# One plain feed-forward block less per layer, with its token sums moved to GpSimd

## The chip, the cores and the metric

The kernel runs on one core of one Trainium2 chip. A core has TensorE (PE, the matrix engine; PEld is its weight load), VectorE (DVE), ScalarE (ACT), GpSimd (POOL) and SyncE (SP), which issues most of the transfers. Each engine works through its own list of instructions in order, and waits on semaphores for the others. The metric is the device time of one execution in microseconds (us), the median of several runs.

## What is computed

Two layers of a decoder trunk over 528 tokens (16 learned meta tokens, then 512 real ones) with a model width of 1024. Each layer has a combined projection, forgetting attention and retention heads, an output projection, and then the part that the change touches, a SwiGLU feed-forward network (FFN) of width 2816:

```
hn = rmsnorm(h, ffn_norm_g)
ff = silu(hn @ w_gate) * (hn @ w_up)
h = h + ff @ w_down
```

After the second layer comes a last norm, and the meta tokens are dropped. All data is float32. Layer 0 works on all 528 tokens in its FFN, layer 1 only on the 512 real ones.

## The kernel before

Activations are held transposed, features on partitions: `h[0..7]` are eight tiles of 128 features by 528 tokens. For precision each float32 operand is split into two float32r tiles, a high part (a cast, on ACT) and a low part (the source less the high part, a subtraction, on DVE or POOL). A product then takes three matmuls: high by high, weight high by activation low, weight low by activation high. So weights arrive by DMA in `raw`, ACT casts them to `whi`, and DVE or POOL subtracts to make `wlo` (`convert`, L165 to L195). A job with `pool` set makes its low parts on POOL, in eight instructions of 128x128; without it DVE makes them in two of 128x512. The high cast of a half (four chunks of 128 rows) always precedes the low parts of that half.

The FFN's 22 blocks of 128 gate and up columns go in rounds (`ROUNDS`, L27): a round makes its blocks' activations, and the next round interleaves the down projection of the round before. There are two kinds of block.

A **plain block** (`dense_steps`, L197) multiplies the eight chunks of the normed input, `xh` and `xl` (made by `scale_split`, L311), by the gate weights in eight steps, and by the up weights in eight more. A step is three matmuls over all tokens, each written as two of 264 columns in layer 0 and one of 512 in layer 1. While a job's steps run, `convert(j + 1, ...)` at steps 1 and 4 makes the two halves of the next job's weights ready.

A **Unit** (L887) computes gate and up for both halves of the tokens with seven half-size products in place of eight, from sums and differences of weight blocks (`make2` to `make4`) and of activation blocks. Each product has four chunks of three matmuls over half of the tokens (264 or 256 columns), 84 matmuls in all. A Unit runs in three parts: head (24 matmuls, needs `xh`, `xl` and the first weights), middle (36, needs the sums `th`, `tl`) and tail (24, needs both).

The activation sums are made once per layer by `x_forms(k)`, k from 0 to 3 (L834), in a buffer `S` of which there are two. ACT scales two token halves of `h[k]` into `S` (L841), four DVE instructions form the four sums (L842 to L845: one subtraction within `S`, three that scale a half of `h[4+k]` and subtract), ACT casts all four to `th`, and DVE makes `tl` (both in `split`, L141). `squares`, `rstd` and `g_done(0)` are inserted between steps as well: the norm's sums of squares, the factor `R` that all later results are scaled by (two matmul pairs at L290, then ACT and DVE), and the first block's gate with its silu, before which ACT loads another function table (L407).

TensorE's order is the order of the program (`manual_schedule`, L1329). For the other engines the framework's scheduler sets the order when the program is built, from the program order, priorities and its own idea of how long things take; on the chip each engine keeps that order even where an instruction in front waits. The first blocks of each layer, f below `PLAIN`, are plain and the other Units. With `PLAIN = 3` the first round, blocks 0 to 2, is plain in whole. Steps counted from 0 at the FFN's start, the x_forms stand ahead of steps 12, 20, 28 and 36, `rstd` ahead of step 12, and the first Unit's head follows the 48 plain steps.

Of the kernel before, what the change touches and what calls it, by code (L numbers as in the profile page):

```python
# [10 lines left out]
F32 = mybir.dt.float32  # L11
F32R = mybir.dt.float32r
AF = mybir.ActivationFunctionType
ALU = mybir.AluOpType

D = 1024
NK = D // 128
# [7 lines left out]
DFF = 2816  # L25
NF = DFF // 128
ROUNDS = ((0, 3), (3, 7), (7, 11), (11, 15), (15, 19), (19, 22))  # L27
PLAIN = 3
HB = NK // 2
EPS = 1e-6  # L30
NBLK = SEQ // 128
# [8 lines left out]
def hybrid_kernel(ctx, tc, x_t, w_in, w_fl, w_out, w_gate, w_up, w_down, vecs, b_fg, rope, decay, mask, ident, out_t):  # L40
    nc = tc.nc
# [9 lines left out]
    h = [state.tile([128, T], F32, name=f"h{k}") for k in range(NK)]  # L51
# [145 lines left out]
    def dense_steps(src, parts, pool=False, banks=False, ahead=(1, 4), own=None, wait=None):  # L197

        j = len(jobs)
        jobs.append({"src": src, "pool": pool, "own": own})

        def chunk(k0, k, n, xs, cols, ps, done):
            def go():
                convert(j)
                if k == 0:
                    t = [psum_a() for _ in cols] if banks else psum()
                    ps.append(t)
                    ps.append(t if banks else [t[:, b] for b in range(2)])  # L210
                size = jobs[j]["w"][0][0]
                _, hi, lo = jobs[j]["w"][(k0 + k) // size]
                wk = (k0 + k) % size
                xh, xl = xs(k)
                for i, (w, x) in enumerate(((hi, xh), (hi, xl), (lo, xh))):
                    for b, (c0, c1) in enumerate(cols):
                        nc.tensor.matmul(ps[1][b][:, 0:c1 - c0], w[:, wk, :], x[:, c0:c1],  # L217
                                         start=(k == 0 and i == 0), stop=(k == n - 1 and i == 2))
                if k == n - 1:
                    done(ps[0]) if wait is None else wait.append(lambda: done(ps[0]))  # L220
                for half, at_step in enumerate(ahead):
                    if k0 + k == at_step:
                        convert(j + 1, 4 * half + 4)
            return go

        steps = []
        for k0, xs, n, cols, done in parts:
            ps = []
            steps += [chunk(k0, k, n, xs, cols, ps, done) for k in range(n)]
        return steps  # L230
# [42 lines left out]
    def fft(tag, dt=F32R, shape=(128, T), bufs=None):  # L273
        return phase["ffn"].tile(list(shape), dt, name=tag, tag=tag, bufs=bufs)
# [72 lines left out]
    def rstd(st, cols, rname="R"):  # L347

        st["R"] = col_rstd(st["parts"], D, cols, rname)
# [443 lines left out]
    def ffn(l, st, real, last):  # L793
        QC = REAL if real else FULL
# [7 lines left out]
        def two(t):  # L802
            return t[:, t0:T].rearrange("p (a b) -> p a b", a=2)
# [4 lines left out]
        def g_done(f):  # L808
            def go(ps):
                sg = tt("sg")  # L810
                if isinstance(ps, list):
                    for v, (c0, c1) in zip(ps, QC):
                        nc.vector.scalar_tensor_tensor(sg[:, c0:c1], v[:, 0:c1 - c0], RSC, st["R"][:, c0:c1],
                                                       ALU.mult, ALU.mult)
                else:
                    nc.vector.scalar_tensor_tensor(sv(sg, real), pv(ps, real), RSC, sv(st["R"], real), ALU.mult, ALU.mult)
                silu(sv(sg, real))
                sgs[f] = sg
            return go

        def u_done(f):
            def go(ps):
                u = tt("tq")
                nc.vector.scalar_tensor_tensor(sv(u, real), pv(ps, real), RSC, sv(st["R"], real), ALU.mult, ALU.mult)
                nc.vector.tensor_mul(sv(u, real), sv(u, real), sv(sgs[f], real))
                fh, fl = act_tile(f)
                split(sv(fh, real), sv(fl, real), sv(u, real))
                acts[f] = (fh, fl)
            return go
# [4 lines left out]
        def x_forms(k):  # L834
            def go():
                if k == 0:
                    st["t"] = [[fft(f"t{p}{i}", shape=(128, 2, 4, w)) for p in "hl"] for i in range(2)]
                s = fft("S", F32, (128, 6, w), 2)
                a, b = ((h[k][:, c0:c1], h[HB + k][:, c0:c1]) for c0, c1 in HC)
                g0, g1 = vcol(V_FFN + l * NK + k), vcol(V_FFN + l * NK + HB + k)  # L840
                nc.scalar.activation(s[:, 0:2], two(h[k]), AF.Copy, scale=g0)  # L841
                nc.vector.tensor_sub(s[:, 2], s[:, 1], s[:, 0])  # L842
                for i in range(2):
                    nc.vector.scalar_tensor_tensor(s[:, 3 + i], b[1], g1, s[:, 1 + i], ALU.mult, ALU.subtract)
                nc.vector.scalar_tensor_tensor(s[:, 5], a[1], g1, s[:, 4], ALU.mult, ALU.subtract)  # L845
                th, tl = (t[:, k % 2] for t in st["t"][k // 2])
                split(th, tl, s[:, 2:6])
            return go
# [180 lines left out]
        for r, (f0, f1) in enumerate(ROUNDS):  # L1029
            for f in range(f0, f1):  # L1030
                if f < PLAIN:
                    steps += dense_steps(w_gate[l, f], [(0, xs, NK, QC, g_done(f) if f else held.append)], banks=f == 1)
                    steps += dense_steps(w_up[l, f], [(0, xs, NK, QC, u_done(f))])
                    continue
                u = Unit(f)
                steps += u.head()
                for v in tails:
                    v.last()
                    steps += v.tail()
                tails = []  # L1040
                u.rest()
                steps += u.middle()
                if fills:
                    p, g0, g1 = fills.pop(0)
                    j = down_job(p, g0, g1)
                    steps += down(j, 0, 2 * p, g0, g1, not real)
                    u.last()
                    steps += u.tail()
                    steps += down(j, 1, 2 * p + 1, g0, g1, False)
                else:  # L1050
                    tails = [u]
            for p, g0, g1 in fills:
                j = down_job(p, g0, g1)
                for s in range(2):
                    steps += down(j, s, 2 * p + s, g0, g1, False)
            fills = [(p, f0, f1) for p in range(NK // 2)]
# [6 lines left out]
        else:  # L1063
# [149 lines left out]
            places = [(end, after_a)] + [(end + n * (i + 1), f) for i, f in enumerate(  # L1213
                (after_0, after_1, after_2, after_3, after_4, after_5, after_6, after_7))]
            steps += merge(rnd, places)
        for i in range(HB):
            steps.insert(NK + 4 + 9 * i, x_forms(i))
        steps.insert(NK + 4, lambda: g_done(0)(held[0]))
        steps.insert(NK + 4, lambda: rstd(st, QC))
        steps.insert(4, lambda: squares(st, QC, False, False))  # L1220
        return steps

    gf = const.tile([128, NK], F32, name="gf")
    nc.vector.tensor_scalar_mul(gf, vec[:, V_FIN:V_FIN + NK], RSC)
# [180 lines left out]
```

## Time and profile before

| what | value |
|---|---|
| median of 3 runs | 1274.08 us (1273.74 to 1275.27) |
| the profiled execution's own time | 1278.19 us |
| its span, first to last instruction | 1276.3 us |
| granted TensorE clock | 0.995 of full speed |
| busy | PE 1258.8, DVE 996.6, ACT 688.2, POOL 265.2 us |
| matmuls | 9271 |

The span is the profiled execution on the chip. A row of a timeline has the start in us from the span's start, the length in us, the engine, the line of the kernel, the operation with what it writes and reads and its size, how many like it follow each other (x), and in brackets how long the engine sat idle before and what ended that. A matmul's row lasts from its start to the end of its pipeline, so neighbours overlap: the pace of TensorE is read from start to start. A row of windows has, for each engine, its busy time in that stretch and in brackets its instructions, then the granted clock. A row of one line's instructions has the shortest, median and longest duration in ns.

### The profile page before, as it was taken

How to read it: one execution, taken by the hardware profiler on the slowest of the kernel's cores; microseconds unless marked ns; L12 is line 12 of the kernel's file. 1: busy time of each engine (PE TensorE's matmuls, PEld its weight loads, DVE VectorE, ACT ScalarE, POOL GpSimd, SP SyncE). 2: the span in 40 equal slices, each digit the busy share in tenths (PEclk: the TensorE clock that was granted, in tenths of full speed). 3: DMA queues.
4: the chain of work that ended last, by engine and by line, in shares of the span. 5: the costliest groups of instructions: out<-in, count | busy, mean ns of one | idle time of the engine just before them, and what ended most of it. 6: DMA issues, size and time to landing. Idle time of an engine off the chain costs nothing.

```text
span 1276.3 us, 23615 instructions
## 1 busy us (share of the span) xinstructions
PE 1258.8 (99%) x9271; PEld 1199.9 (94%) x9271; DVE 996.6 (78%) x1843; ACT 688.2 (54%) x1246; POOL 265.2 (21%) x522
## 2 busy tenths in 40 slices
PE   9999999999999999999999999999999999999997
PEld 8899999999999999999998989999789999999996
DVE  7777856779988887887785777567899888888866
ACT  6666545676444444444464665456764444444444
POOL 3355546420000000000025545554100000000000
PEclk9999999999999999999999999999999999999998
DMA  6322232223333333332323232232224333333321
GB/s 216 93 68 84 79 94 72 74 67 112 108 96 100 100 100 100 100 100 83 102 74 100 76 100 84 75 92 67 99 86 129 100 100 100 100 99 101 106 76 67
DMA packets 45680, 120.57 MB, mean 94 GB/s; under 512 B 5360, under 2 KB 12272, under 8 KB 45568
## 3 DMA queue, kind: packets, MB, share of 16 engines
q1 hardware_dynamic: 45136, 118.77, 29.8%
q8 instruction: 73, 1.20, 0.4%
q14 instruction: 39, 0.32, 0.1%
q10 hardware_dynamic: 432, 0.29, 0.1%
HBM read 116.91 MB, written 2.13 MB: 93 GB/s over the span
## 4 chain that ended last, share of the span: by engine, by line
PE 94%; DVE 2%; ACT 1%; DMA 1%; issue 0%; DVEq 0%; ACTq 0%; SPq 0%
PE psd L217 30%; PE psa L880 18%; PE psd L1015 14%; PE psd L880 13%; PE psa L217 5%; PE psa L1015 4%; PE psa L418 2%; PE psa L572 2%; PE psa L507 2%; PE psa L729 1%; PE psa L699 1%; DMA bc<-cdr 1%; PE psa L379 1%; PE psa L290 0%; DMA cdr<-z 0%
## 5 line engine op out<-in xcount | busy, mean ns | idle before, releaser
L194 POOL TENSOR_TENSOR wlo<-raw,whi 128x128 fp32r<-128x128 f32 x504 | 259.9, 551 | 293.5 <-ACT whi L191 293.5
L217 PE MATMUL psd<-xh,whi 128*128 128x264 f32 (+1 forms) x792 | 197.1, 316 | 0.6 <-ACT whi L191 0.6
L217 PE MATMUL psd<-xh,wlo 128*128 128x264 f32 (+1 forms) x792 | 187.7, 305 | 0.0
L217 PE MATMUL psd<-xl,whi 128*128 128x264 f32 (+1 forms) x792 | 187.3, 304 | 0.4 <-DVE xl L320 0.4
L217 PEld LDWEIGHTS psd<-xh,whi 128*128 128x128 f32 x792 | 129.4, 191 | 5.7 <-ACT whi L191 1.3
L217 PEld LDWEIGHTS psd<-xh,wlo 128*128 128x128 f32 x792 | 128.0, 190 | 6.4 <-DVE wlo L194 0.4
L217 PEld LDWEIGHTS psd<-xl,whi 128*128 128x128 f32 x792 | 128.6, 190 | 4.8 <-DVE xl L320 0.8
L191 ACT CAST whi<-raw 128x512 fp32r<-128x512 f32 (+1 forms) x168 | 98.5, 614 | 51.6 <-PE psd L217 38.2
L868 ACT CAST whi<-raw 128x1024 fp32r<-128x1024 f32 (+2 forms) x62 | 54.9, 886 | 51.0 <-PE psd L880 39.5
L868 ACT CAST fwhi<-raw 128x1024 fp32r<-128x1024 f32 (+2 forms) x62 | 55.7, 898 | 46.6 <-PE psd L880 39.2
L1115 POOL TENSOR_TENSOR th<-th,e 128x544 f32<-128x544 f32 x1 | 1.4, 1370 | 359.1 <-DVE e L1135 359.1
L85 POOL MEMSET kl<- 64x528 f32 x2 | 1.1, 534 | 345.4 <-PE psa L880 345.4
L869 DVE TENSOR_TENSOR wlo<-raw,whi 128x1024 fp32r<-128x1024 f32 (+2 forms) x62 | 62.9, 1015 | 12.1 <-ACT whi L868 12.0
L869 DVE TENSOR_TENSOR fwlo<-raw,fwhi 128x1024 fp32r<-128x1024 f32 (+2 forms) x62 | 64.0, 1032 | 9.6 <-ACT fwhi L868 9.5
L880 PE MATMUL psa<-th,whi 128*128 128x264 f32 (+1 forms) x232 | 65.4, 282 | 0.0
L880 PE MATMUL psa<-th,wlo 128*128 128x264 f32 (+1 forms) x232 | 65.4, 282 | 0.0
L880 PE MATMUL psa<-tl,whi 128*128 128x264 f32 (+1 forms) x232 | 65.3, 282 | 0.0
L880 PE MATMUL psa<-th,fwhi 128*128 128x264 f32 (+1 forms) x224 | 63.4, 283 | 0.0
L880 PE MATMUL psa<-tl,fwhi 128*128 128x264 f32 (+1 forms) x224 | 63.3, 283 | 0.0
L880 PE MATMUL psa<-th,fwlo 128*128 128x264 f32 (+1 forms) x224 | 63.2, 282 | 0.0
L527 ACT ACTIVATE probs<-probs,nmax 128x144 f32<-128x144 f32 (+1 forms) x64 | 36.9, 577 | 47.3 <-DVE nmax L514 34.5
L868 ACT CAST fwhi<-S 128x1024 fp32r<-128x1024 f32 x20 | 21.0, 1050 | 69.1 <-PE psa L880 67.1
(340 smaller groups left out, 4053.7 us busy)
## 6 DMA issues: line engine op xcount, KB each, us to landing
raw<-w_in SPq DMA_DIRECT2D x54, 512.0 KB, 3.5
raw<-w_gate SPq DMA_DIRECT2D x44, 512.0 KB, 3.8
fraw<-w_up SPq DMA_DIRECT2D x38, 512.0 KB, 3.5
raw<-w_down SPq DMA_DIRECT2D x64, 256.0 KB, 2.8
raw<-w_out SPq DMA_DIRECT2D x16, 512.0 KB, 3.4
raw<-w_down SPq DMA_DIRECT2D x32, 192.0 KB, 2.5
bc<-cdr SPq DMA_DIRECT2D x16, 264.0 KB, 3.4
raw<-w_up SPq DMA_DIRECT2D x6, 512.0 KB, 3.6
```

Of the source, the lines that this page charges most:

```text
L191: pin(nc.scalar.copy(hi, job["raw"][:, c0:c1]), pinned)
L194: pin(sub(lo[:, i:i + step], job["raw"][:, c0 + i:c0 + i + step], hi[:, i:i + step].bitcast(F32)), pinned)
L217: nc.tensor.matmul(ps[1][b][:, 0:c1 - c0], w[:, wk, :], x[:, c0:c1], start=(k == 0 and i == 0), stop=(k == n - 1 and i == 2))
L379: nc.tensor.matmul(ps[:, 0:c1 - c0], wf[:, k, :], st["x"][k][part][:, c0:c1], start=(i == 0), stop=(i == 2 * NK - 1))
L418: nc.tensor.transpose(ps[:, 128 * j:128 * j + 128], src[:, o:o + 128], idt)
L507: nc.tensor.matmul(sc[0:nq, 0:c1 - c0], st["q"][s][:, q0:q0 + nq], kk[:, c0:c1], start=(i == 0), stop=(i == 1))
L527: nc.scalar.activation(pr, pr, AF.Exp, bias=nmax[0:nq], scale=-1.0, accum_out=rsum)
L572: nc.tensor.matmul(po[:, c0:SEQ], v[:, j, :], pp[:, j, META + c0:T], start=(j == 0 and i == 0), stop=(j == 4 and i == 1))
L868: nc.scalar.copy(hi, src)
L869: nc.vector.tensor_sub(lo, src, hi.bitcast(F32))
L880: nc.tensor.matmul(bank()[:, 0:b.shape[-1]], a[:, o + k, :], b, start=(fresh and k == 0 and i == 0), stop=(k == n - 1 and i == 2), skip_gr ...
L1015: nc.tensor.matmul(v[:, 0:c1 - c0], a[:, s * n + k, :], b[:, c0:c1], start=(k == 0 and i == 0), stop=(k == n - 1 and i == 2))
```

## The change

`PLAIN` becomes 2: block 2 of each layer is now a Unit too, the first round has two plain blocks and a Unit, and that Unit's head follows 32 plain steps. Of the plain blocks' four weight jobs all but the first get `pool` set, so POOL makes their low parts. In `x_forms` ACT scales both `h[k]` and `h[4+k]` into a larger `S`, and all four sums become POOL subtractions. The x_forms stand ahead of steps 7, 11, 15 and 19, and `rstd` and `g_done(0)` ahead of step 11.

```diff
-PLAIN = 3
+PLAIN = 2
...
-                s = fft("S", F32, (128, 6, w), 2)
-                a, b = ((h[k][:, c0:c1], h[HB + k][:, c0:c1]) for c0, c1 in HC)
+                s = fft("S", F32, (128, 8, w), 2)
                 g0, g1 = vcol(V_FFN + l * NK + k), vcol(V_FFN + l * NK + HB + k)
                 nc.scalar.activation(s[:, 0:2], two(h[k]), AF.Copy, scale=g0)
-                nc.vector.tensor_sub(s[:, 2], s[:, 1], s[:, 0])
+                nc.scalar.activation(s[:, 6:8], two(h[HB + k]), AF.Copy, scale=g1)
+                nc.gpsimd.tensor_sub(s[:, 2], s[:, 1], s[:, 0])
                 for i in range(2):
-                    nc.vector.scalar_tensor_tensor(s[:, 3 + i], b[1], g1, s[:, 1 + i], ALU.mult, ALU.subtract)
-                nc.vector.scalar_tensor_tensor(s[:, 5], a[1], g1, s[:, 4], ALU.mult, ALU.subtract)
+                    nc.gpsimd.tensor_sub(s[:, 3 + i], s[:, 7], s[:, 1 + i])
+                nc.gpsimd.tensor_sub(s[:, 5], s[:, 6], s[:, 4])
...
-                    steps += dense_steps(w_gate[l, f], [(0, xs, NK, QC, g_done(f) if f else held.append)], banks=f == 1)
-                    steps += dense_steps(w_up[l, f], [(0, xs, NK, QC, u_done(f))])
+                    steps += dense_steps(w_gate[l, f], [(0, xs, NK, QC, g_done(f) if f else held.append)], f > 0, f == 1)
+                    steps += dense_steps(w_up[l, f], [(0, xs, NK, QC, u_done(f))], True)
...
-        for i in range(HB):
-            steps.insert(NK + 4 + 9 * i, x_forms(i))
-        steps.insert(NK + 4, lambda: g_done(0)(held[0]))
-        steps.insert(NK + 4, lambda: rstd(st, QC))
-        steps.insert(4, lambda: squares(st, QC, False, False))
-        return steps
+        forms = (7, 11, 15, 19)
+        return merge(steps, [(4, lambda: squares(st, QC, False, False)), (NK + 3, lambda: rstd(st, QC)),
+                             (NK + 3, lambda: g_done(0)(held[0]))], [(p, x_forms(i)) for i, p in enumerate(forms)])
```

The change's lines after `x_forms` are one to three numbers lower than before's; here lines are before's unless a row of the change is shown. Its two ACT scalings are L840 and L841, and its sums L842 to L845 as before.

On GpSimd, at the start of layer 0's FFN, the piece of the difference in which the token sums come in. The `wlo` rows are low parts of weights, eight to a job; the 256 end with those of the first up job, and the later groups of four belong to the second gate job:

```order
-L194 TENSOR_TENSOR wlo<-raw,whi 128x128 x248
-L85 MEMSET kl_8409 64x528
-L85 MEMSET kl_8410 64x528
+L194 TENSOR_TENSOR wlo<-raw,whi 128x128 x256
+L842 TENSOR_TENSOR S<-S 128x264
+L844 TENSOR_TENSOR S<-S 128x264 x2
+L845 TENSOR_TENSOR S<-S 128x264
+L842 TENSOR_TENSOR S<-S 128x264
+L844 TENSOR_TENSOR S<-S 128x264 x2
+L194 TENSOR_TENSOR wlo<-raw,whi 128x128 x4
+L845 TENSOR_TENSOR S<-S 128x264
+L194 TENSOR_TENSOR wlo<-raw,whi 128x128 x4
```

Before, GpSimd had no work there until the next layer's memsets; now it has 24 low parts and 16 sums in the FFN's beginning, mixed in one queue. Behind this piece stand the sums of k = 2, the first sum of k = 3, four low parts of the second up job, two sums, one low part, the last sum, and three low parts.

On ScalarE at the same place, before. `sqh` is the high part of the norm's sum of squares, `R` the norm's factor, `sg` the first gate, and each `x2` of L191 the two halves of one weight job:

```order
L841 ACTIVATE S<-h_74,vec 128x528
L142 CAST sqh<-ss 128x528
L191 CAST whi<-raw 128x512 x2
L295 ACTIVATE R<-psa,epsc 128x264 x2
L142 CAST th_4303<-S 128x1056
L296 ACTIVATE R<-R 128x528
L142 CAST th_4303<-S 128x1056
L191 CAST whi<-raw 128x512 x2
```

On ScalarE now, from the first cast of k = 2's sums to the weights of the first Unit. `ah` is the high part of the first block's product:

```order
L142 CAST th_4256<-S 128x1056
L191 CAST whi<-raw 128x512
L841 ACTIVATE S<-h_80,vec 128x528
L191 CAST whi<-raw 128x512
L142 CAST th_4256<-S 128x1056
L407 ACT_TABLE_LOAD
L407 ACTIVATE sg<-sg 128x528
L868 CAST fwhi<-S 128x1024
L142 CAST ah_4375<-tq 128x528
L868 CAST whi<-raw 128x1024
```

The two L191 rows here are the second up job's high parts. They stand behind the cast of k = 2's sums, and the first Unit's weights (the last row) behind the cast of k = 3's sums, the table load, the first silu, and two more casts.

On VectorE now, from the last low part of the sums to the low parts of the first Unit's weights (the last row):

```order
L143 TENSOR_TENSOR tl_4257<-S,th_4256 128x1056
L915 TENSOR_TENSOR S<-S,raw 128x512
L825 TENSOR_TENSOR tq<-tq,sg 128x528
L921 TENSOR_TENSOR fraw<-raw,fraw 128x512
L813 SCALAR_TENSOR_TENSOR sg<-psa,R 128x264 x2
L143 TENSOR_TENSOR al_4376<-tq,ah_4375 128x528
L869 TENSOR_TENSOR fwlo<-S,fwhi 128x1024
L869 TENSOR_TENSOR wlo<-raw,whi 128x1024
```

Before, only one row stood between the last `tl` and this `wlo`; now six do, the first silu's result among what they wait for. In layer 1 the change puts this `wlo`, and its cast on ScalarE, ahead of the `al` and `fwlo` rows, and keeps the sums of squares' cast behind k = 0's `th`; otherwise the queues are alike.

## The prediction

> **What bounds the kernel now.** I read the page first, then TensorE's timeline at both FFN starts, then windows there, then the other engines' timelines. The page's span, busy time and chain:
>
> ```profile
> span 1276.3 us, 23615 instructions
> PE 1258.8 (99%) x9271; PEld 1199.9 (94%) x9271; DVE 996.6 (78%) x1843; ACT 688.2 (54%) x1246; POOL 265.2 (21%) x522
> PE 94%; DVE 2%; ACT 1%; DMA 1%; issue 0%; DVEq 0%; ACTq 0%; SPq 0%
> ```
>
> TensorE is the bound, so a matmul less is time less, and a wait put into TensorE is time more. Where the change acts, windows of 20 us in the plain blocks of layer 0 and of layer 1 show TensorE without a gap, VectorE full too, GpSimd empty:
>
> ```profile
> 292.00:312.00 20.00, 20.00 (x166) 19.85 (x165) 19.96 (x37) 12.61 (x20) 0.00 (x0) 1.00 0.40 136
> 925.00:945.00 20.00, 20.00 (x87) 16.25 (x88) 19.69 (x36) 12.64 (x19) 0.00 (x0) 1.00 0.32 98
> ```
>
> TensorE's timeline: the first plain step, the Unit's first and twelfth matmul, in each layer.
>
> ```profile
> 290.02 0.41 PE L217 MATMUL psd<-xh,whi 128*128 128x264 f32 x2
> ...
> 325.56 0.28 PE L880 MATMUL psa<-xh,whi 128*128 128x264 f32 x1
> ...
> 326.89 0.28 PE L880 MATMUL psa<-xh,wlo 128*128 128x264 f32 x1
> ...
> 918.08 0.40 PE L217 MATMUL psd<-xh,whi 128*128 128x512 f32 x1
> ...
> 952.61 0.28 PE L880 MATMUL psa<-xh,whi 128*128 128x256 f32 x1
> ...
> 953.92 0.28 PE L880 MATMUL psa<-xh,wlo 128*128 128x256 f32 x1
> ```
>
> **Part one: a plain block becomes a Unit.** In layer 0, 35.54 us hold three blocks of 96 matmuls and the four of L290: 0.1217 each, a block 11.68. Eleven starts of a Unit take 1.33, 0.121 each, so its 84 cost 10.16: 1.52 less. In layer 1 a block is at most a third of 34.53; the window's 87 in 20 us give 0.230 each, and its 48 cost 11.04. A Unit's pace there is 1.31 / 11 = 0.119, and 84 cost 10.0: 1.04 less. Together **-2.6**. Without a wait the first Unit would start one block sooner, at 313.88 and 941.57; its third matmul, which needs the first low part on VectorE, comes two starts later, at 314.12 and 941.81.
>
> **Part two: what GpSimd gets.** Its low parts free and beside VectorE, VectorE's own subtraction with and without GpSimd beside it, GpSimd's one other large subtraction-like instruction, and VectorE beside that; then VectorE's price for a sum:
>
> ```profile
> L194 POOL TENSOR_TENSOR wlo<-raw,whi x504: 447/463/2071, 21.9 to 902.8; 128x128 fp32r<-128x128 f32 x168
> ...
> 21.95 3.39 POOL L194 TENSOR_TENSOR wlo<-raw,whi 128x128 fp32r<-128x128 f32 x8 [20.26 <-ACT whi L191]
> 267.57 2.18 POOL L194 TENSOR_TENSOR wlo<-raw,whi 128x128 fp32r<-128x128 f32 x4 [8.38 <-ACT whi L191]
> 268.07 0.94 DVE L297 TENSOR_TENSOR nwt<-r 128x528 f32<-128x528 f32 x1 [0.37 <-ACT r L296]
> 302.60 0.70 DVE L297 TENSOR_TENSOR nwt<-R 128x528 f32<-128x528 f32 x1
> ...
> 1262.10 0.40 DVE L1111 TENSOR_TENSOR S<-S,sq 128x240 f32<-128x240 f32 x1
> 1262.35 1.37 POOL L1115 TENSOR_TENSOR th<-th,e 128x544 f32<-128x544 f32 x1 [359.05 <-DVE e L1135]
> 1262.73 1.25 DVE L1111 TENSOR_TENSOR S<-S,sq 128x240 f32<-128x240 f32 x1
> ...
> L842 DVE TENSOR_TENSOR S<-S x8: 418/424/429, 297.5 to 938.4; 128x264 f32<-128x264 f32 x4, 128x256 f32<-128x256 f32 x4
> ```
>
> A free low part costs 3.39 / 8 = 0.424. A sum is not in the trace: it lies between 0.424 (as if 264 columns were 128) and 0.463 x 264 / 128 = 0.955 (as if nothing were fixed). On the line through 128 columns (0.463) and 544 (1.37) it is 0.76, and 0.04 less back to back: I take **0.72**, 0.70 for 256 columns. [...]
>
> The two engines also hold each other up. A VectorE instruction with both inputs in SBUF took 0.94 beside GpSimd where it takes 0.70, and one of 0.40 took 1.25, until GpSimd's 1.37 was over; four low parts beside it took 2.18, not 1.70. L299, with an input in PSUM, I count as free of this. So I add the two engines' times where both have such work. [...]
>
> **Part three: the queues at layer 0's start.** The ACT and VectorE rows that I price with:
>
> ```profile
> 289.98 1.15 ACT L191 CAST whi<-raw 128x512 fp32r<-128x512 f32 x2 [0.63 <-PE psd L217]
> 291.03 0.74 ACT L841 ACTIVATE S<-h,vec 128x528 f32<-128x528 f32 x1
> ...
> 300.31 1.07 ACT L142 CAST th<-S 128x1056 fp32r<-128x1056 f32 x1
> ...
> 305.26 1.28 ACT L407 ACT_TABLE_LOAD   x1
> 307.62 0.65 ACT L407 ACTIVATE sg<-sg 128x528 f32<-128x528 f32 x1 [1.08 <-DVE sg L816]
> ...
> 319.78 1.06 ACT L868 CAST whi<-raw 128x1024 fp32r<-128x1024 f32 x1 [1.09 <-issue]
> ```
>
> ```profile
> 291.09 2.12 DVE L320 SCALAR_TENSOR_TENSOR xl<-h,vec,xh 128x528 fp32r<-128x528 f32 x3
> ...
> 301.42 1.26 DVE L143 TENSOR_TENSOR tl<-S,th 128x1056 fp32r<-128x1056 f32 x1
> ...
> 309.61 0.70 DVE L825 TENSOR_TENSOR tq<-tq,sg 128x528 f32<-128x528 f32 x1
> ...
> 310.83 0.43 DVE L813 SCALAR_TENSOR_TENSOR sg<-psa,R 128x264 f32<-128x264 f32 x1
> 311.17 0.70 DVE L143 TENSOR_TENSOR al<-tq,ah 128x528 fp32r<-128x528 f32 x1
> ...
> 319.19 1.25 DVE L143 TENSOR_TENSOR tl<-S,th 128x1056 fp32r<-128x1056 f32 x1
> ...
> 320.98 1.22 DVE L869 TENSOR_TENSOR wlo<-raw,whi 128x1024 fp32r<-128x1024 f32 x1
> 322.11 0.69 DVE L915 TENSOR_TENSOR S<-S,raw 128x512 f32<-128x512 f32 x1
> ```
>
> GpSimd starts when the up job's first half is cast, 290.55. To its last sum stand 21 low parts, 21 x 0.424 = 8.9, and 16 sums, 16 x 0.72 = 11.5: 20.4. On the shared time lie five `xl`, one `ss` and `sql` on VectorE, some 0.66 each (4.6), later a `tl` of 1.2, half of another, two instructions for `R` and one for the Unit's weights (3.7): 8.3. GpSimd also waits for ACT: for k = 1's second scaling, which stands behind k = 0's cast (1.07 + 0.74 less the 0.72 that GpSimd has to do), for k = 2's (0.7), and for the second up job's high part, behind k = 2's cast (1.07 + 0.57 less 0.72): 2.7. The last sum ends at 290.55 + 20.4 + 8.3 + 2.7 = 321.95.
>
> From there, by the queues shown: on ACT cast 1.07, table load 1.28, silu 0.65, 3.0 in all (`tl` and L915 are done by then); on VectorE L825, L921, two L813, `al`, `fwlo`, `wlo`, 0.70 + 0.69 + 0.86 + 0.70 + 1.22 + 1.22 less overlaps, 5.1; ACT's 1.06 for `fwhi`, 0.65 and 1.06 end before. The Unit's third matmul comes at 321.95 + 8.1 = 330.05, against 314.12: **+15.9**. Part of it shows sooner, as waits of the second up job for its high parts, which stand behind k = 2's cast.
>
> Layer 1: GpSimd starts at 918.65 by the like cast; own work 8.9 + 16 x 0.70 = 20.1; shared 6 x 0.66 + 3.0 = 7.0; waits 2.7; the last sum at 948.45. There `wlo` stands ahead of `al` and `fwlo`, so the tail is 3.0 + three instructions of 0.62 + 1.22 = 6.1: 954.55 against 941.81, **+12.7**. L290 waits there too, since the squares' cast stands behind k = 0's, but GpSimd's queue ends later and covers that.
>
> **The clock.** The only longer gap that TensorE has shows what follows one:
>
> ```profile
> 683.42 0.41 PE L418 MATMUL psa<-idt,vt 128*128 128x128 f32 x1 [1.80 <-DVE vv L484]
> 683.48 0.78 PE L217 MATMUL psd<-xh,whi 128*128 128x512 f32 x1
> 684.05 0.63 PE L217 MATMUL psd<-xl,whi 128*128 128x512 f32 x1
> 684.48 0.63 PE L217 MATMUL psd<-xh,wlo 128*128 128x512 f32 x1
> ...
> 686.99 0.40 PE L217 MATMUL psd<-xh,whi 128*128 128x512 f32 x1
> ```
>
> ```profile
> 683.50:686.90 3.40, 3.40 (x11) 2.92 (x12) 2.81 (x10) 0.72 (x2) 0.00 (x0) 0.50 0.43 147
> ```
>
> After 1.80 us of idling the starts lie 0.43 apart, not 0.23, until 686.99, and the granted clock of that window is 0.50. 3.4 us at half pace lose 1.7; once a layer, behind the last wait, that is **+3.4**. Earlier such losses lie inside the waits for GpSimd.
>
> **What is free.** ACT's added scalings, 8 of 0.74, are in the waits above. SP's loads move by a row or two, and TensorE does not wait for one now. VectorE's relief, 16 sums and six half low parts a layer, is worth nothing, since TensorE did not wait for it. The new Unit's product is needed some 6 us behind its tail (36 matmuls of the next Unit and 12 of the down projection, 0.12 each), where block 2's had a head more; I count nothing, and at most 0.4 a layer in the range.
>
> **Sum.** -2.6 + 15.9 + 12.7 + 3.4 = +29.4 on the profiled execution's 1278.2, so 1307.6. Its own time lies 4.1 over the runs' median, 1274.1; I forecast 1303.5. This kernel's measurement can tell 0.2%, 2.5 us, from no change.
>
> **The rivals.**
> - *No sharing.* GpSimd and VectorE do not delay each other here; for it speaks that many low parts keep the median of 463 ns, against it the 1.25 and 2.18. Then 8.3 and 7.0 go: 29.4 - 15.3 = +14, 1288.
> - *Cheap sums.* A sum costs 0.424 and nothing is shared: 16 x 0.30 less again in a layer, +4 to +5, 1279. Against it stands the 1.37.
> - *All hidden, faster.* TensorE's work decides: -2.6, 1271.5. This needs the last sum 8.1 before 314.12, at 306.0: 21 low parts and 16 sums in 15.45, so a sum of at most 0.41 with no wait at all, about VectorE's own 0.424. The other engines' slack speaks for it, every GpSimd row against.
> - *Just covered.* The waits come to 1.3 a layer and eat the gain: 1274.
> - *Sums not sooner.* The places in the program are sooner, but by the queues they end later, 324.3 for the last `tl` (321.95 + 1.07 + 1.26), where before's row above ends at 320.4; this is my forecast itself.
>
> **Chances.** Forecast 0.64 (its own range 1295 to 1313: a sum of 0.955 adds 16 x 0.235 x 2 = 7.5, and the late product 0.8), no sharing 0.19, cheap sums 0.06, all hidden 0.07, just covered 0.04. The range takes the first two: 1286 to 1313, 0.83. Slower 0.88, with most of cheap sums; same 0.05; faster 0.07.
>
> **What would show it.** GpSimd's L842 to L845 at 0.7 or more each, longer where VectorE's `xl` and `tl` run; ACT idle before `th` for GpSimd's S; TensorE idle at the second up job for `whi` and at the first Unit for `wlo`, over 10 us a layer, with a half-clock stretch behind. Sums under 0.5, or TensorE without a gap until the first Unit, would prove me wrong.

## The result and the profile after

The change makes the kernel slower: 1304.07 us median of 4 runs (1302.4 to 1305.29), against 1274.67 (1273.74 to 1276.19) for the kernel before beside it, a ratio of 1.0229 with a 95% interval of 1.0211 to 1.0246. The forecast was 1303.5. The profiled execution's own time is 1304.02, its span 1302.2, its granted clock 0.988.

The page of the change, span, busy times and chain:

```profile
span 1302.2 us, 23752 instructions
PE 1264.3 (97%) x9295; PEld 1202.9 (92%) x9295; DVE 993.5 (76%) x1813; ACT 696.7 (54%) x1260; POOL 321.9 (25%) x602
PE 84%; DVE 6%; POOL 3%; ACT 3%; DMA 2%; issue 1%; ACTq 0%; DVEq 0%; SPq 0%; POOLq 0%
```

TensorE's share of the chain falls from 94% to 84%, and GpSimd, absent before, holds 3%. Where it happens, the windows at the start of layer 0's FFN show (columns as before: length, PE, PEld, DVE, ACT, POOL, granted clock):

```profile
290.00:310.00 20.00, 16.65 (x132) 15.93 (x131) 9.24 (x11) 9.64 (x16) 18.73 (x27) 1.00 0.29 107
310.00:330.00 20.00, 12.60 (x71) 12.21 (x72) 15.10 (x20) 11.04 (x14) 8.14 (x13) 0.74 0.08 23
```

VectorE was full before (19.96 of 20) and now does 9.24: it waits. The full engine is GpSimd, 18.73 of 20. In the second window TensorE has gaps and the granted clock drops to 0.74. TensorE's timeline, with the first plain step of layer 0, its longest wait, the Unit's third matmul, and the same for layer 1, where L290 waits as well (layer 1's attention part starts at 661.15):

```profile
287.86 0.41 PE L217 MATMUL psd<-xh,whi 128*128 128x264 f32 x2
...
315.40 0.78 PE L217 MATMUL psd<-xh,whi 128*128 128x264 f32 x2 [7.35 <-DVE sg L816]
...
325.92 0.39 PE L880 MATMUL psa<-xh,wlo 128*128 128x264 f32 x1 [1.91 <-DVE wlo L869]
...
661.15 0.40 PE L217 MATMUL psd<-xh,whi 128*128 128x512 f32 x1
...
928.96 0.40 PE L217 MATMUL psd<-xh,whi 128*128 128x512 f32 x1
...
940.90 0.71 PE L290 MATMUL psa<-sqh,ones 128*128 128x512 f32 x1 [2.61 <-ACT sqh L142]
...
955.42 0.77 PE L217 MATMUL psd<-xh,whi 128*128 128x512 f32 x1 [2.94 <-DVE sg L816]
...
965.29 0.39 PE L880 MATMUL psa<-xh,wlo 128*128 128x256 f32 x1 [1.07 <-DVE wlo L869]
```

From first plain step to first plain step the span divides into stages. Before, layer 1's attention part starts here:

```profile
647.81 0.40 PE L217 MATMUL psd<-xh,whi 128*128 128x512 f32 x1
```

| stage | before | after | difference |
|---|---|---|---|
| up to layer 0's FFN | 290.02 | 287.86 | -2.2 |
| layer 0's FFN | 357.79 | 373.29 | +15.5 |
| layer 1's attention part | 270.27 | 267.81 | -2.5 |
| layer 1's FFN and the end | 358.22 | 373.24 | +15.0 |

The two FFNs take 30.5 more. The attention parts, which the change does not touch, differ for the most part by TensorE's pace in two short stretches (last section); together they are about the 4.1 by which the profiled execution of before lay over its median.

GpSimd in layer 0, from the first up job's low parts to the last sum and the three low parts behind it, and then the line that ends each form (a form is one `x_forms`), with who waited for it:

```profile
288.57 6.74 POOL L194 TENSOR_TENSOR wlo<-raw,whi 128x128 fp32r<-128x128 f32 x8 [16.49 <-ACT whi L191]
295.27 0.75 POOL L842 TENSOR_TENSOR S<-S 128x264 f32<-128x264 f32 x1
...
300.11 1.90 POOL L844 TENSOR_TENSOR S<-S 128x264 f32<-128x264 f32 x2 [1.11 <-ACT S L841]
301.97 1.70 POOL L194 TENSOR_TENSOR wlo<-raw,whi 128x128 fp32r<-128x128 f32 x4
...
304.34 2.75 POOL L194 TENSOR_TENSOR wlo<-raw,whi 128x128 fp32r<-128x128 f32 x4
...
312.20 3.16 POOL L194 TENSOR_TENSOR wlo<-raw,whi 128x128 fp32r<-128x128 f32 x4 [1.00 <-ACT whi L191]
...
317.14 0.75 POOL L845 TENSOR_TENSOR S<-S 128x264 f32<-128x264 f32 x1
317.85 1.29 POOL L194 TENSOR_TENSOR wlo<-raw,whi 128x128 fp32r<-128x128 f32 x3
```

```profile
L845 POOL TENSOR_TENSOR S<-S x8: 723/735/757, 297.5 to 958.4; 128x264 f32<-128x264 f32 x4, 128x256 f32<-128x256 f32 x4
...
  ACT th L142: 31.4, 8
```

A sum takes 0.75, eight low parts beside VectorE's `xl` 6.74 in place of 3.39, and ScalarE stands idle 31.4 us in front of the eight `th` casts. VectorE's queue inherits this. Its rows up to the `sg` for which TensorE waits 7.35:

```profile
299.43 1.26 DVE L143 TENSOR_TENSOR tl<-S,th 128x1056 fp32r<-128x1056 f32 x1 [4.43 <-ACT th L142]
305.52 1.26 DVE L143 TENSOR_TENSOR tl<-S,th 128x1056 fp32r<-128x1056 f32 x1 [4.83 <-ACT th L142]
307.42 0.96 DVE L297 TENSOR_TENSOR nwt<-R 128x528 f32<-128x528 f32 x1 [0.65 <-ACT R L296]
308.41 0.77 DVE L299 SCALAR_TENSOR_TENSOR nwt<-psa,nwt 128x264 f32<-128x264 f32 x2
311.63 1.26 DVE L143 TENSOR_TENSOR tl<-S,th 128x1056 fp32r<-128x1056 f32 x1 [2.45 <-ACT th L142]
312.81 0.96 DVE L300 SCALAR_TENSOR_TENSOR R<-nwt,R 128x528 f32<-128x528 f32 x1
313.69 0.94 DVE L914 TENSOR_TENSOR S<-fraw 128x512 f32<-128x512 f32 x1
314.56 0.70 DVE L816 SCALAR_TENSOR_TENSOR sg<-psd,R 128x528 f32<-128x528 f32 x1
```

The second up job needs a `psd` buffer, of which there are two; the first gate's product holds one until this `sg` has read it. `sg` needs `R`, and `R`'s last step stands behind k = 2's `tl`, which waits for ScalarE's cast, which waits for GpSimd. The wait bears VectorE's name, its cause is three queues back.

### The profile page after: what moved, and what is told of

The parts are those of the page before. It is cut to its first block, busy times and chain, and to the rows that moved or that the text cites. A ratio compares the mean times of both kernels' runs of the same rounds, so it can differ in the third digit from the quotient of the medians.

```text
span 1302.2 us, 23752 instructions
## 1 busy us (share of the span) xinstructions
PE 1264.3 (97%) x9295; PEld 1202.9 (92%) x9295; DVE 993.5 (76%) x1813; ACT 696.7 (54%) x1260; POOL 321.9 (25%) x602
## 4 chain that ended last, share of the span: by engine, by line
PE 84%; DVE 6%; POOL 3%; ACT 3%; DMA 2%; issue 1%; ACTq 0%; DVEq 0%; SPq 0%; POOLq 0%
PE psd L217 24%; PE psa L880 18%; PE psd L1015 14%; PE psd L880 12%; PE psa L1015 4%; PE psa L217 4%; PE psa L418 2%; POOL wlo L194 2%; PE psa L572 2%; PE psa L507 1%; PE psa L729 1%; PE psa L699 1%; POOL S L844 1%; PE psa L379 1%; DVE fwlo L869 1%
## 5 line engine op out<-in xcount | busy, mean ns | idle before, releaser
L194 POOL TENSOR_TENSOR wlo<-raw,whi 128x128 fp32r<-128x128 f32 x552 | 291.1, 562 | 321.9 <-ACT whi L191 321.8
L217 PE MATMUL psd<-xh,whi 128*128 128x264 f32 (+1 forms) x744 | 185.8, 318 | 10.5 <-DVE sg L816 10.3
L217 PE MATMUL psd<-xl,whi 128*128 128x264 f32 (+1 forms) x744 | 176.2, 305 | 1.6 <-DVE xl L320 1.6
L217 PE MATMUL psd<-xh,wlo 128*128 128x264 f32 (+1 forms) x744 | 175.4, 304 | 0.0
L217 PEld LDWEIGHTS psd<-xh,whi 128*128 128x128 f32 x744 | 122.2, 192 | 15.7 <-issue 7.5
L217 PEld LDWEIGHTS psd<-xl,whi 128*128 128x128 f32 x744 | 121.2, 191 | 7.0 <-DVE xl L320 3.6
L217 PEld LDWEIGHTS psd<-xh,wlo 128*128 128x128 f32 x744 | 120.6, 190 | 5.3
L191 ACT CAST whi<-raw 128x512 fp32r<-128x512 f32 (+1 forms) x160 | 93.8, 612 | 45.5 <-PE psd L217 33.7
L869 DVE TENSOR_TENSOR wlo<-raw,whi 128x1024 fp32r<-128x1024 f32 (+2 forms) x64 | 64.3, 1004 | 13.3 <-ACT whi L868 13.2
L880 PE MATMUL psa<-th,whi 128*128 128x264 f32 (+1 forms) x248 | 69.9, 282 | 1.1 <-ACT e L946 1.1
L946 ACT COPY e<-psa 128x264 f32<-128x264 f32 (+1 forms) x120 | 45.0, 375 | 30.5 <-PE psa L880 26.2
```

Source lines behind the costliest of these rows:

```text
L191: pin(nc.scalar.copy(hi, job["raw"][:, c0:c1]), pinned)
L194: pin(sub(lo[:, i:i + step], job["raw"][:, c0 + i:c0 + i + step], hi[:, i:i + step].bitcast(F32)), pinned)
L869: nc.vector.tensor_sub(lo, src, hi.bitcast(F32))
L880: nc.tensor.matmul(bank()[:, 0:b.shape[-1]], a[:, o + k, :], b, start=(fresh and k == 0 and i == 0), stop=(k == n - 1 and i == 2), skip_gr ...
L946: nc.scalar.copy(self.t["e"][:, i], self.t["x"][:, 0:w])
```

## The experiments

**Theory.** GpSimd's one queue of 24 low parts and 16 sums, lengthened by what GpSimd and VectorE take from each other (eight low parts in 6.74 us, not 3.39), runs late; ScalarE's casts and VectorE's rows behind them inherit that, and TensorE waits in the second plain block and at the first Unit. A "shared port" in the expectations is the author's name for this taking; the runs show what it costs, not where in the hardware it arises. **Rivals:** B, one of the two kinds of work is the whole cost; C, the Unit cannot be fed 11.7 us sooner whoever does the work; F, the PSUM buffer or the order on VectorE is the cost.

First the change with one kind of work, or both, given back to VectorE. **Sums on VectorE:**

```diff
...
-                nc.gpsimd.tensor_sub(s[:, 2], s[:, 1], s[:, 0])
+                nc.vector.tensor_sub(s[:, 2], s[:, 1], s[:, 0])
...
-                    nc.gpsimd.tensor_sub(s[:, 3 + i], s[:, 7], s[:, 1 + i])
+                    nc.vector.scalar_tensor_tensor(s[:, 3 + i], b[1], g1, s[:, 1 + i], ALU.mult, ALU.subtract)
...
```

> The change, but the sixteen token sums of a layer go back to VectorE in the form of the kernel before (0.424 us each there); the low parts stay on GpSimd, the first round stays two plain blocks and a Unit, the places stay sooner. Theory A (GpSimd's mixed queue of 24 low parts and 16 sums sets the first Unit's start): GpSimd has only 8.9 us of low parts up to the last sum, so its part of the wait goes; VectorE takes 16 x 0.424 = 6.8 us a layer back, some 26 us of work ahead of the first Unit against 24 us of TensorE work, so 0 to 6 us of waiting a layer are left: 1272 to 1284 us. Rival B (the low parts of the plain blocks are the cost): little changes, 1297 or more. Rival C (a Unit 11.7 us sooner cannot be fed by ScalarE and VectorE, whoever makes the sums): 1290 or more, with ScalarE never waiting for GpSimd's S.

Measured: 1287.12, ratio to before 1.0089 (1.0077 to 1.0102). More than half of the loss goes, less than A expected.

**Low parts on VectorE:**

```diff
-                    steps += dense_steps(w_gate[l, f], [(0, xs, NK, QC, g_done(f) if f else held.append)], f > 0, f == 1)
-                    steps += dense_steps(w_up[l, f], [(0, xs, NK, QC, u_done(f))], True)
+                    steps += dense_steps(w_gate[l, f], [(0, xs, NK, QC, g_done(f) if f else held.append)], banks=f == 1)
+                    steps += dense_steps(w_up[l, f], [(0, xs, NK, QC, u_done(f))])
```

> The change, but the plain blocks' weight low parts go back to VectorE; the sums stay on GpSimd. Theory A: GpSimd's queue loses 21 x 0.424 = 8.9 us and some of the shared time, VectorE gains six halves of two low parts (7.4 us a layer): of about 15 us of waiting a layer 4 to 8 are left, 1282 to 1292 us. Rival B (the low parts are the cost): no waiting left, 1272 to 1275. Rival C (the Unit cannot be fed sooner, whoever does it): as the change, 1298 or more.

Measured: 1290.77, 1.0116 (1.0102 to 1.013), as A expected. B falls: with either kind alone on GpSimd some 40 to 50% of the 29.4 stays, so neither is the whole cost.

**Both on VectorE:**

> The change with both kinds of work back on VectorE, sums and low parts: two plain blocks and the sooner places alone, GpSimd empty there. Theory A (the first Unit waits for the longest queue): VectorE then has some 33 us ahead of the first Unit against 24 of TensorE, 8 to 10 us of waiting a layer, 1288 to 1292 us; better than the change, worse than with either half on GpSimd. Rival C (the sooner Unit is the cost whoever does the work): 1300 or more. If GpSimd's queue were the only cost: 1272.

Measured: 1290.24, 1.0108 (1.0092 to 1.0123). A's number, though not A's order (the run with the sums on GpSimd is no quicker), and C in part: without GpSimd 14.5 us stay. In this kernel's windows VectorE has hardly a gap, and TensorE has:

```profile
293.00:313.00 20.00, 18.83 (x152) 18.25 (x151) 20.00 (x39) 12.25 (x18) 0.00 (x0) 1.00 0.22 74
313.00:333.00 20.00, 17.93 (x146) 17.50 (x145) 19.94 (x28) 10.89 (x16) 0.00 (x0) 1.00 0.30 93
```

In the plain blocks and Units TensorE waits most for VectorE's `wlo` (3.0 us in all), then for ScalarE's `fwhi` (2.6) and `ah` (2.3). A full VectorE is the likely reason for the 14.5; that it is the only one is not shown.

**The kernel before with the sums alone on GpSimd** (the change's `x_forms`, nothing else):

> The kernel before (three plain blocks, old places, low parts on VectorE) with one edit: the sums go to GpSimd and ScalarE scales both halves, as in the change. Theory A: a GpSimd sum still costs 0.72 or more, but it stands alone in its queue and the first Unit comes 11.7 us later than in the change, so TensorE does not wait: 1272 to 1277 us. Rival D (a sum on GpSimd makes each form's chain too long wherever it stands, its four sums of 0.75 with ScalarE's second scaling in front of every cast): 5 us or more a layer, 1284 or more.

Measured: 1288.46, 1.0094 (1.0078 to 1.0109). The theory's number is wrong and rival D's right: 11.7 us more room does not cover GpSimd's sums. Whether the chain that D names is the cost is open, since what the two engines take from each other can cost as much (13.3 us in the next run). ScalarE waits for the sums there, in us, times and longest:

```profile
ACT th L142 <- POOL S L845: 17.8, 8, 3.1
```

The next run was made to see why. It puts sixteen subtractions a layer on GpSimd for which **nobody waits**, beside VectorE's own sums:

```diff
+                d = fft("D", F32, (128, 4, w), 1)
+                for i in range(4):
+                    c0, c1 = HC[i % 2]
+                    nc.gpsimd.tensor_sub(d[:, i], h[k][:, c0:c1], h[HB + k][:, c0:c1])
```

> The kernel before, and beside it sixteen GpSimd subtractions a layer of the sums' size (h[k] less h[4+k], half of the tokens each), four at each form, into a tile that nothing reads: no engine waits for them, so only what the two engines take from each other costs. Shared-port theory: VectorE is full there (19.69 of 20 us in the kernel before) and loses some 0.3 to 0.6 us to each, 5 to 9 us a layer, of which TensorE's slack of a few us swallows a part: 4 to 16 us in all, 1280 to 1292 us. Without sharing: 1275 to 1278, no wait of TensorE that the kernel before has not.

Measured: 1288.77, 1.0101 (1.0085 to 1.0116), 13.3 us for work that nothing reads. ScalarE's and VectorE's instructions stand in the same order as before at both FFN starts, so no queue was rearranged. TensorE's largest wait, the subtraction's durations (ns), three `xl` of VectorE beside it and a subtraction of VectorE of the same size alone, then windows of layer 0, the second behind the waits:

```profile
PE psd L217 <- DVE xl L320: 7.1, 7, 2.0
...
L849 POOL TENSOR_TENSOR D<-h,h x32: 721/1188/1273, 280.8 to 932.6; 128x264 f32<-128x264 f32 x16, 128x256 f32<-128x256 f32 x16
...
293.81 3.67 DVE L320 SCALAR_TENSOR_TENSOR xl<-h,vec,xh 128x528 fp32r<-128x528 f32 x3
297.41 1.25 DVE L340 TENSOR_TENSOR ss<-ss,sq 128x528 f32<-128x528 f32 x1
...
300.43 0.70 DVE L143 TENSOR_TENSOR sql<-ss,sqh 128x528 fp32r<-128x528 f32 x1
```

```profile
288.00:299.00 11.00, 7.33 (x46) 6.13 (x44) 11.00 (x12) 5.15 (x9) 10.84 (x10) 0.92 0.39 143
...
297.15:303.95 6.80, 6.06 (x26) 5.45 (x26) 6.39 (x10) 1.77 (x3) 2.12 (x2) 0.50 0.11 16
```

Both engines look busy to the brim, but each finishes one instruction in 1.2 us (3.60 / 3 on VectorE, a median of 1.188 on GpSimd) where alone they take 0.70 and 0.72: they nearly take turns. No engine waits for these subtractions, so that is what the two engines take from each other, and it costs as much as GpSimd's real sums did. Only a part of the 13.3 is waiting: TensorE idles 7.1 for `xl`, and the granted clock is 0.50 for 6.8 us in each layer behind that. TensorE works 6.06 of them in layer 0 and 5.26 in layer 1, which at half pace loses, by estimate, another 5.7. These subtractions ran some microseconds sooner than the change's sums, beside `xl`; the size carries over only roughly.

**The places alone**, three plain blocks and all on VectorE:

> The kernel before (three plain blocks, sums and low parts on VectorE) with the sooner places alone. Theory A (the places only reorder ScalarE's and VectorE's queues; the cost of the change without GpSimd is that the first Unit comes 11.7 us sooner): 1274 to 1279 us. Rival C2 (the sooner places hold up R and the second plain block): 1285 or more, as the change without GpSimd's work had 1290.

Measured: 1279.07, 1.0022 (1.0012 to 1.0031). At the upper end of what A expected; the places are a small cost, not a gain.

**The change with three plain blocks:**

```diff
-PLAIN = 2
+PLAIN = 3
...
-                    steps += dense_steps(w_gate[l, f], [(0, xs, NK, QC, g_done(f) if f else held.append)], f > 0, f == 1)
-                    steps += dense_steps(w_up[l, f], [(0, xs, NK, QC, u_done(f))], True)
+                    steps += dense_steps(w_gate[l, f], [(0, xs, NK, QC, g_done(f) if f else held.append)], f == 1, f == 1)
+                    steps += dense_steps(w_up[l, f], [(0, xs, NK, QC, u_done(f))], f < 2)
```

> The change with three plain blocks (block 2 plain as before, its low parts on VectorE): sums and 24 low parts a layer on GpSimd, sooner places. If the first Unit's start alone decides, as my prediction priced it (ready 43.8 us after layer 0's FFN start in the prediction, some 39.6 in the change's trace, against 35.5 of TensorE work), 4 to 6 us of waiting are left over both layers, 1279 to 1283 us. If GpSimd's queue holds up TensorE already before the Unit (the second up job, which stands at the same place here), the waits of the change's second block stay, 8.7 in layer 0 and 6 in layer 1 with some half-clock time behind them: 1290 to 1296 us.

(Its 43.8 and 39.6 are misread: by the rows quoted, the third matmul of the Unit comes 40.0 after the FFN's start in the prediction and 38.1 in the change. The bound that it draws from them changes little.) Measured: 1301.86, 1.0193 (1.0179 to 1.0207), beyond both. Block 2 is plain again, and 25 of the 29 us stay. TensorE's wait is where it was in the change, and as long:

```profile
315.78 0.78 PE L217 MATMUL psd<-xh,whi 128*128 128x264 f32 x2 [7.32 <-DVE sg L816]
```

The first Unit waits for nothing here: its third matmul comes 48.94 and 45.99 after the FFN's start (337.18 - 288.24 and 975.84 - 929.85), 13.2 and 11.2 later than without a wait, all of it lost before the Unit. So the waits in the second plain block are hard costs of their own; here they are not a share, shown early, of a wait that the Unit would have anyway.

**One kind of work with three plain blocks,** first the low parts:

> Three plain blocks, sooner places, the sums on VectorE, only the low parts of blocks 0 and 1 on GpSimd (24 a layer). From the run with two plain blocks, where low parts on GpSimd gained 3 us over all on VectorE, and the run of the sooner places alone (1279): if the low parts relieve VectorE, 1275 to 1278; if the shared port takes back more than the relief where TensorE had no wait, 1280 to 1284.

Measured: 1280.03, 1.0035 (1.0022 to 1.0048), at the lower edge of the second range; over the places alone it is too little to tell. And the sums:

> Three plain blocks, sooner places, only the sums on GpSimd, low parts on VectorE. As with the old places (1288): 1286 to 1291 if the chain of GpSimd's sum, ScalarE's th and VectorE's tl, all in order, is what costs; 1280 or less if the old places were a part of it. The sum of what sums alone and low parts alone cost, against the 1302 of both, says how much comes from the two standing in one queue.

Measured: 1287.54, 1.0094 (1.008 to 1.0107), as with the old places. That fits the chain and the taking of turns alike; the run does not separate them. All eight, in us over the kernel before measured beside each, sooner places throughout, each uncertain by 1 to 2:

| on GpSimd | three plain blocks | two plain blocks |
|---|---|---|
| nothing | +2.5 | +14.5 |
| low parts | +4.5 | +11.3 |
| sums | +12.0 | +15.0 |
| both | +25.3 | +29.4 |

With three plain blocks the sums add 9.5 and the low parts 2.0, both together 22.8: 11.3 come only with the two in one queue (half-clock stretches behind the longer waits included: behind the 7.32 at 315.78 pairs of matmuls start 0.44 apart). With two, where VectorE is full, each alone costs about what VectorE doing it costs (-3.2 and +0.5), and both add 14.9. The missing block costs 12.0 where VectorE does all and 4.1 where GpSimd does both: the waits overlap, and no single part owns the 29.4.

**The PSUM wait.** The second up job's product into the single banks, so that no `sg` must come first:

```diff
...
-                    steps += dense_steps(w_up[l, f], [(0, xs, NK, QC, u_done(f))], True)
+                    steps += dense_steps(w_up[l, f], [(0, xs, NK, QC, u_done(f))], True, f == 1)
```

VectorE then reads that product in two instructions, one for each bank.

> The change, but the second up job writes into the single PSUM banks (psa), so it need not wait until VectorE's first sg has emptied a psd bank; that is the wait of 7.4 us in layer 0 and 2.9 in layer 1. Theory A (the release is late only because all queues run behind GpSimd's sums): the wait moves to the second up job's low parts and to the first Unit's wlo, total within 3 us of the change, 1301 to 1305 us. Rival F (VectorE's order, with sg behind k = 2's tl, is the cost): 8 to 10 us go, 1294 to 1296.

Measured: 1305.66, 1.0225 (1.0211 to 1.0239): nothing gained, F falls. TensorE's waits in layer 0 there:

```profile
315.18 0.81 PE L217 MATMUL psa<-xh,whi 128*128 128x264 f32 x2 [4.11 <-ACT whi L191]
326.54 0.39 PE L885 MATMUL psa<-xh,whi 128*128 128x264 f32 x1 [2.30 <-ACT whi L873]
328.96 0.59 PE L885 MATMUL psa<-xh,wlo 128*128 128x264 f32 x1 [1.91 <-DVE wlo L874]
```

With the buffer free the same job waits 4.11 for its high part, which stands behind k = 2's cast, and the Unit gives back the rest: its third matmul comes 38.11 and 36.37 after the FFN's start (328.96 - 290.85 and 968.32 - 931.95), in the change 38.06 and 36.33. In the change the wait for the buffer is thus a share of the Unit's wait. With three plain blocks the buffer was not freed; how much of the 25.3 it costs there is open.

**A fifth sum:**

```diff
+                nc.gpsimd.tensor_sub(s[:, 1], s[:, 6], s[:, 0])
```

> The change with a fifth GpSimd subtraction of the same size in each of the four forms of a layer, whose result nothing reads; ScalarE's and VectorE's queues keep their order. Theory A (GpSimd's queue sets when the middle of the plain blocks and the first Unit can run): 4 x 0.75 = 3.0 us a layer on GpSimd, up to 4 with what it holds up on VectorE: 6 to 8 us more than the change, 1310 to 1313 us. Rival E (GpSimd has slack and VectorE's or ScalarE's own queue sets it): 0 to 2 us more.

Measured: 1308.11, 1.0244 (1.023 to 1.0257), against the change's 1.0229: 1.9 us more, with intervals that overlap. That number lies in E's range, not in A's. By the traces layer 0's FFN takes 375.46 in place of 373.29, 2.2 more, and the last sum ends 31.5 us after GpSimd's start there, not 29.3. Of 3.0 us more in the queue some 2.2 arrive, in part because one low part (0.45) that the change has ahead of the last sum stands behind it here. Layer 1's FFN takes 1.3 more. The trace shows A's direction with less than half of A's size, and the times alone do not exclude E.

## Why the prediction was right

*The Unit's saving, -2.6.* Nothing measured contradicts it, and 48 matmuls of the new Unit start 0.121 apart (330.23 to 335.92) as priced; but no run shows the saving by itself, since with two plain blocks there was always a wait.

*GpSimd's own work, 20.4.* A sum was priced 0.72 and took 0.75 (L845's median 0.735). The nearest pair of rows, 128 and 544 columns, had given it.

*The shared time, 8.3, and GpSimd's waits for ScalarE, 2.7.* The last sum ended at 317.88, 29.3 after GpSimd's start, where 31.4 was forecast. Its idle time was 1.11 and 1.00, so 2.1; what is left over 20.4 and 2.1 is 6.8 for the shared time and the little that the sums took above 0.72. Both terms right in kind, 1.5 and 0.6 too long. L299, counted as free, took 0.77 for two beside GpSimd's low parts (269.05 before) and 0.77 without them (304.38). The run of unread subtractions shows that the rival without sharing (1288) was wrong in kind.

*The tail, 8.1.* From the last sum at 317.88 to the end of `wlo` at 325.87: 8.0, in the order of queues that was worked out.

*The stalls, 15.9 and 12.7.* The Unit's third matmul stands 38.06 (325.92 - 287.86) and 36.33 (965.29 - 928.96) after the FFN's start, 14.0 and 12.6 over the 24.10 and 23.73 without a wait. Right in size and, for the change, in the way it was counted: at the Unit, with what comes sooner as a part of it. The run with other banks shows this, for there the earlier wait is shorter and the third matmul comes at the same 38.1 and 36.4. Wrong was what the earlier wait is. The prediction took it for a wait for `whi`; the one that ended last was for the PSUM buffer, by way of `sg` and `R`, a release that I had not followed (`whi` was the next to come). And I had not seen that this wait is nearly as long by itself. With three plain blocks the reckoning at the Unit leaves some 4 us (38.06 and 36.33 against 35.78 and 34.77 with a block more), and 25 stayed. In the change the Unit's wait ends later by only what TensorE still idles there, 1.91 and 1.07 us; the prediction had not weighed the two against each other, so that its one was the later was luck.

*Unstalled at 314.12.* The step "VectorE's relief is worth nothing" fits the change, where VectorE idles. It can't be said in general: with the same work on VectorE 14.5 us are lost, so the Unit would not have started at 314.12 there either. No run has cheap sums on GpSimd, so what the rivals "cheap sums", "just covered" and "all hidden" assume was not met (a sum took 0.75), and where they would have ended is open.

*The clock, +3.4.* Layer 0 has the half-clock stretch behind its last wait, 1.7. In layer 1 none follows the Unit; the stretches there lie inside the waits. 1.7, not 3.4. The window in layer 0:

```profile
326.60:330.00 3.40, 3.40 (x18) 3.40 (x17) 3.40 (x6) 0.38 (x1) 0.00 (x0) 0.50 0.02 5
```

*The late product, 0, at most 0.4 a layer.* Too low. Block 2's `al` and, in layer 1, an eviction by ScalarE and VectorE's sum into `h` come late:

```profile
347.60 0.52 PE L1015 MATMUL psa<-al,fwhi 128*128 128x264 f32 x2 [0.92 <-DVE al L143]
...
972.10 0.39 PE L880 MATMUL psa<-th,whi 128*128 128x256 f32 x1 [1.05 <-ACT e L946]
...
986.40 0.50 PE L1015 MATMUL psd<-al,fwhi 128*128 128x512 f32 x1 [0.92 <-DVE al L143]
...
1032.70 0.50 PE L1015 MATMUL psd<-ah,whi 128*128 128x512 f32 x1 [0.47 <-DVE h L1022]
```

With the slower start behind each (347.60 to 347.96 is 0.36 for a pair that else takes 0.24), I estimate 1.1 in layer 0 and some 3 in layer 1 (the idle times alone are 0.9 and 2.4).

*The sum.* By stages: layer 0: -1.5 + 14.0 + 1.7 + 1.1 = 15.3 of 15.5. Layer 1: -1.0 + 12.6 + 3 = 14.6 of 15.0. The forecast had 16.1 and 13.4: a stall 1.9 too long in layer 0, and late products in layer 1 in place of a half-clock stretch. That the errors cancel to 1 us is luck. That the 4.1 by which the profiled execution lay over the median should be taken off again was right: it sits in stages without the change.

## What to carry to other kernels

Work moved to an engine that is idle is not free where that engine and the one it relieves hold each other up, as here, where one instruction of each took 1.2 us and alone 0.72 and 0.70: price the pair as taking turns, with the half-clock stretch that a wait can leave behind (0.50 for 3.40 us behind the change's wait of 1.91), and ask first whether the relieved engine is what the bound engine waits for. Where an in-order queue runs late, look for every transfer, cast and buffer release that stands behind it, on the other engines too; the wait will carry the name of the last of them (here 7.35 us under that of `sg`). And before pricing one engine's queue against an unstalled start, check that the others could have fed that start: with all of the work on VectorE half of the loss was still there.

## What the runs showed of the hardware

A short gap of TensorE sometimes halves its clock and sometimes not. The prediction's stretch behind a gap of 1.80 us had a granted clock of 0.50. The same place in the change has a gap of 1.70 and a clock that stays at 1.00, which saved its profile 1.7 us there:

```profile
695.84 0.30 PE L418 MATMUL psa<-idt,vt 128*128 128x128 f32 x1 [1.70 <-DVE vv L484]
```

The length of the gap alone is not what decides: at the end of the kernel before, a gap of 1.26 us ahead of the matmul at 1265.73 is followed by a granted clock of 0.50 from 1267.15. In the change's profile the clock changes at 312.97, 319.80, 326.62, 330.04, 941.02 and so on, whole multiples of 3.41 us apart. Three windows of that grid, laid on each profile's own changes: before's that ends with the gap of 1.80, then the change's two around the gap of 1.70:

```profile
680.06:683.47 3.41, 1.02 (x7) 0.50 (x6) 1.99 (x9) 2.18 (x8) 1.70 (x4) 1.00 0.13 49
...
691.87:695.28 3.41, 2.26 (x13) 1.72 (x11) 1.99 (x9) 2.54 (x9) 1.70 (x4) 1.00 0.48 194
695.28:698.69 3.41, 2.85 (x16) 2.45 (x17) 3.38 (x12) 0.85 (x4) 0.00 (x0) 1.00 0.48 154
```

Before, one window holds the whole gap, TensorE is busy for 1.02 of it, and the next window is the prediction's stretch at 0.50. In the change the grid cuts the gap in two, and neither window falls below 2.26. Over these two profiles in whole, the windows at full clock in which TensorE was busy for 0 to 1.41 us (five: 680.06 before; 309.56, 323.21, 937.61 and 951.26 in the change) were all followed by half clock, and those with 2.26 or more never; of the three between, 1.90 (306.14 in the change) was not, 2.09 (1263.73 before and 1289.18 in the change) was both times. So here a half-clock stretch behind a short gap went with how much of one window the gap took, not with its length alone, and it can't be counted on either way.

At the program's beginning the pace doubled some 5 us sooner in the change. Before, pairs of matmuls start 0.44 apart until 11.03:

```profile
10.59 0.61 PE L217 MATMUL psd<-xh,wlo 128*128 128x264 f32 x2
11.03 0.41 PE L217 MATMUL psd<-xh,whi 128*128 128x264 f32 x2
11.28 0.41 PE L217 MATMUL psd<-xl,whi 128*128 128x264 f32 x2
```

In the change the next pair follows after 0.28 already at 5.71:

```profile
5.71 0.44 PE L217 MATMUL psd<-xl,whi 128*128 128x264 f32 x2
5.99 0.40 PE L217 MATMUL psd<-xh,wlo 128*128 128x264 f32 x2
```

In the change such pairs start 0.44 apart from 316.42 to 319.06 too, where the granted clock is 0.50, and 0.24 apart from 319.88 on, where it is 1.00. That the clock was halved at the beginning is read from the pace alone: the windows there give 1.00 throughout, but the traces' records of the clock begin only at 11.04 and 5.77.

In the run of unread subtractions GpSimd and VectorE did little at the same time: alone an instruction lasts 0.72 and 0.70, beside each other one of each takes 1.2. And GpSimd loses as well as VectorE: eight low parts of 3.39 us took 6.74 in the change.
